# The state recurrence of a gated linear-attention branch, re-associated: factors formed for four chunks at once

## The chip, the cores and the metric

One Trainium2 chip, one of its cores. The metric is the time of one execution in microseconds of device time; the median of three runs is taken. The engines are named as the profile names them: PE is the matrix engine (PEld its weight loads), DVE the vector engine, ACT the scalar engine, POOL GpSimd, SP the queue that issues most transfers.

## The reference

A decoder layer of width 1024 over 1024 tokens. One input projection feeds three branches (a recurrence of 16 heads of 64, a causal convolution of width 31, a cross-attention into 256 tokens); each is projected, they are merged by sigmoid gates, and one output projection and a residual follow. Only the recurrence matters here:

```
def wkv7_scan(r, decay, k, v, a_vec, b_vec):
    def step(state, inp):
        r_t, w_t, k_t, v_t, a_t, b_t = inp
        sa = einsum('bhvk,bhk->bhv', state, a_t)
        state = (state * w_t[:, :, None, :] + sa[..., :, None] * b_t[:, :, None, :]
                 + v_t[..., :, None] * k_t[:, :, None, :])
        y = einsum('bhvk,bhk->bhv', state, r_t)
        return state, y
...
    wkv = wkv7_scan(rh, decay, kh, vh, -kk, kk * ah)     # then a norm per head, a bonus term, a gate
```

## The kernel before

The products of the layer ("dense" work) are 128x128 by 128x512 matmuls at line 291. Every operand is split into two parts of reduced precision, and three products of parts stand for one, so that an output tile of 128 features by 512 tokens takes 24 of them. The order in which an engine gets its instructions is chosen when the kernel is built: a scheduler starts from the order of the program and may bring ready work forward.

The recurrence is cut into units (a pair of heads j, a half e of the tokens); a unit has 8 chunks of 64 tokens. There are 16 units. Three generators work on one, each in a later period than the one ahead:

- `g_prep` (lines 454 to 549) forms decays, the scaled A and R (tile `ar`), the scaled B and K (tile `bk`) and, for each chunk, head and row, the products of `bk` with `ar` (line 541), masked by DVE at line 543 into the tile `g`. In `g` a chunk has four 64x64 blocks for each head: B with A, K with A, B with R, K with R. For even and odd chunks the halves of the 128 partitions are swapped (`own` and `oth`).
- `g_sub` (lines 552 to 613) inverts the triangular B-with-A block. The 32x32 diagonal blocks are inverted by 31 small steps on DVE (lines 575 and 578), through scratch in DRAM on both sides; two rounds of 32x32 matmuls (lines 600 and 609) make the off-diagonal block. The result T stands in `g`, in place of the block.
- `g_chain` (lines 618 to 719) walks the chunks. For four chunks at a time (q = 0, 1) it transposes `bk` (line 628, tile `tk`) and V (line 635, tile `sav`). For each chunk: line 655 multiplies the state S by A and R into a bank `ry`; line 658 adds the K-with-A block times V for each head; ACT copies this to `rhs` (661); line 669 multiplies by T; ACT copies the result beside V into `sav` (670); line 676 multiplies `tk` by `sav` for each head, and DVE makes the new state from it (679); line 683 adds the B-with-R and K-with-R blocks times `sav` for each head to `ry`, and ACT copies that to `Y` (684). The norm and the gate follow at lines 692 to 718.

A period runs a list of dense tiles (three as a rule) beside the chain of one unit, the `g_sub` of the next and the `g_prep` of the one after. `mix` (line 305) advances these generators over 60 slots, in proportion to a number of steps given for each: 12 for a dense tile (4 matmuls each), `CHN + 2 * GNW` = 30 for a chain. Accumulators are banks of PSUM: two for `d` (dense), two for `g`, two for `ry`, one for `tr`, one for `sas`.

After the last unit the attention, the convolution and the merge follow; the change does not touch them.

Of the kernel before, what the change touches and what calls it, by code (L numbers as in the profile page):

```python
# [18 lines left out]
P = 128  # L19
# [5 lines left out]
C = 64  # L25
# [4 lines left out]
CHN = 28  # L30
# [14 lines left out]
# tiles of the packed weights  # L45
# [5 lines left out]
# columns of the packed per-feature vectors  # L51
# [11 lines left out]
def hybrid_kernel(ctx: ExitStack, tc: tile.TileContext, x: bass.AP, mem: bass.AP, wt: bass.AP,  # L63
# [10 lines left out]
    def bank(tag, bufs=1):  # L74
        return ps.tile([P, HS], F32, name=tag, tag=tag, bufs=bufs)

# [35 lines left out]
    # rsqrt of (in * mul + add) on tiny tiles  # L112
# [17 lines left out]
    # weights stream through in a fixed order: load two tiles ahead, split one tile ahead  # L130
# [34 lines left out]
    # periods of the RWKV pipeline: dense tiles, and what runs beside them in which part of the period  # L165
# [17 lines left out]
    # jobs of the attention and convolution phase: a pair of GLU tiles now and then, so that the taps  # L183
    # of the convolution run beside all of it
# [47 lines left out]
    # RMSNorm of rows, transposed to [feature, token] and split  # L232
# [32 lines left out]
    # a spilled [feature, token] array, back and split  # L265
# [38 lines left out]
    # advance generators side by side; each has its number of steps and its window of the period  # L304
# [15 lines left out]
    # the first tile of products begins beside the norm of the second half of the tokens  # L320
# [7 lines left out]
    # =================== RWKV ===================  # L328
    with tc.tile_pool(name="rk", bufs=1, reuse_waits="tile") as rk:
        # Chunks of 64 tokens; chunk c keeps its own rows at partitions so = 64 * (c even) and the  # L330
        # rows of V, K, R and Y at the other half, so that two chunks fill the 128 partitions.
# [6 lines left out]
        # masks over [rows s, columns t]: strict (s < t) in the columns of A, s <= t in those of R  # L338
# [43 lines left out]
        # low-rank inputs tanh(w_lo) and a_lo: the high parts in rows 0-63, the low parts in rows 64-127  # L382
# [62 lines left out]
        # sums over the features of each head  # L445
# [8 lines left out]
        def g_prep(j, e):  # L454
# [80 lines left out]
            for par in range(2):  # L535
                for hh in range(2):
                    gp = bank("g", 2)
                    rows = slice(hh * C, (hh + 1) * C)
                    for cc in range(4):
                        c = 2 * cc + par  # L540
                        pe.matmul(gp[:, cc * P:(cc + 1) * P], lhsT=fl(bk[rows, c, :, :]), rhs=fl(ar[rows, c, :, :]),  # L541
                                  start=True, stop=True)
                    dve.tensor_tensor(out=g[:, par, hh, :, :], in0=gp.rearrange("p (c t) -> p c t", t=P),  # L543
                                      in1=cmask[par][:, None, :].broadcast_to([P, 4, P]), op=ALU.mult)
                    yield
# [6 lines left out]
        def g_sub(j, e):  # L552
            un = (2 * j + e) % 2
            g = GG[j, e]
            U = rk.tile([NG * 32, 32, 32], F32, name="U", tag="U", bufs=2)
# [28 lines left out]
            t11 = rk.tile([P, 8, 32], F32, name="t11", tag="t11")  # L584
# [33 lines left out]
        def g_chain(j, e):  # L618
# [582 lines left out]
```

## Time and profile before

| | before |
|---|---|
| median of three runs | 2046.52 us (2045.52 to 2048.74) |
| span of the profiled execution | 2042.7 us |
| PE busy | 1999.4 us, 98% of the span, 11140 matmuls |
| DVE busy | 1340.9 us, 66% |
| ACT busy | 730.0 us, 36% |
| POOL busy | 232.1 us, 11% |
| share of 16 DMA engines, main queue | 28.0% |

The span runs from the first to the last instruction of one execution that was profiled. No whole time is listed for that execution: the three timed runs are 2.8 to 6.0 us longer than its span, and that is what lies around it. A matmul's duration in the rows includes the time that it spends in the array's pipeline, so that two neighbours overlap: what one takes from the engine is read from start to start. An fp32 matmul at lines 541 to 683 appears as two instructions in the rows, a transpose or a dense product as one.

### The profile page before, as it was taken

Reading aid. Unit: us, or ns where it says so; the run is one execution under the profiler, and the core shown is the slowest. Engines: PE = TensorE matmul, PEld = TensorE weight load, DVE = VectorE, ACT = ScalarE, POOL = GpSimd, SP = SyncE. Lnnn points to the kernel's source line nnn. Section 1 sums busy time; section 2 is a strip of 40 time slices with the busy share of each in tenths; the row PEclk is TensorE's granted clock in tenths of the full one; section 3 lists DMA queues with packets and bytes.
Section 4 is the critical chain, followed back from the end, with each engine's and each line's share of the span. In section 5 each row is a group of like instructions: output and inputs, shape, how many; then the busy total and the mean of one; then the engine's idle time right before and its main releaser. Section 6 shows DMA issues by size and latency. Waiting matters only on the chain.

```text
span 2042.7 us, 29527 instructions
## 1 busy us (share of the span) xinstructions
PE 1999.4 (98%) x11140; PEld 1558.9 (76%) x11140; DVE 1340.9 (66%) x2802; ACT 730.0 (36%) x1495; POOL 232.1 (11%) x311
## 2 busy tenths in 40 slices
PE   7999999999999999999999999999999999899998
PEld 5777777777777777777777888888888777678887
DVE  6664676656667566675632798989899857654423
ACT  6324344443434434343333432332313335432221
POOL 2201201111011111111100000000000132200001
PEclk9999999999999999999999999999999999999999
DMA  4221212212121221212221432112122566795432
GB/s 141 75 79 50 63 42 59 59 50 74 28 74 43 58 65 29 78 45 65 59 63 64 155 99 62 52 52 73 62 70 75 180 212 195 227 295 176 127 133 83
DMA packets 127936, 188.59 MB, mean 92 GB/s; under 512 B 64433, under 2 KB 66609, under 8 KB 127793
## 3 DMA queue, kind: packets, MB, share of 16 engines
q1 hardware_dynamic: 122704, 178.11, 28.0%
q10 hardware_dynamic: 4768, 8.07, 1.1%
q8 instruction: 87, 1.43, 0.3%
q0 software_dynamic: 320, 0.52, 0.1%
q14 instruction: 57, 0.46, 0.1%
HBM read 139.92 MB, written 46.20 MB: 91 GB/s over the span
## 4 chain that ended last, share of the span: by engine, by line
PE 79%; DVE 9%; DMA 5%; issue 3%; ACT 2%; POOL 2%; SPq 0%; DVEq 0%; POOLq 0%; ACTq 0%
PE d L291 55%; PE d L212 4%; PE g L541 3%; PE ry L658 2%; PE sas L669 2%; DVE ac L795 2%; PE sas L676 2%; DVE wl L124 2%; DMA ost<-o_rwkv_d 1%; PE ry L683 1%; PE ry L655 1%; POOL vr L118 1%; PE g L212 1%; PE ry L212 1%; DMA wf<-in_wt_dram 1%
## 5 line engine op out<-in xcount | busy, mean ns | idle before, releaser
L291 PE MATMUL d<-hH,wh 128*128 128x512 f32 x1552 | 632.1, 407 | 5.1 <-DVE cg L882 3.6
L291 PE MATMUL d<-hH,wl 128*128 128x512 f32 x1552 | 629.8, 406 | 0.0
L291 PE MATMUL d<-hL,wh 128*128 128x512 f32 x1552 | 623.0, 401 | 0.0
L291 PEld LDWEIGHTS d<-hH,wh 128*128 128x128 f32 x1552 | 292.9, 189 | 67.0 <-DVE cg L882 4.8
L291 PEld LDWEIGHTS d<-hH,wl 128*128 128x128 f32 x1552 | 292.7, 189 | 64.6 <-issue 0.2
L291 PEld LDWEIGHTS d<-hL,wh 128*128 128x128 f32 x1552 | 293.0, 189 | 57.3
L795 DVE SCALAR_TENSOR_TENSOR ac<-up,wdw,ac 128x1024 f32<-128x1024 f32 x240 | 307.7, 1282 | 11.8 <-ACT ac L792 5.9
L123 ACT CAST wh<-wf 128x1024 fp32r<-128x1024 f32 x137 | 143.5, 1048 | 291.1 <-PE d L291 270.1
L124 DVE TENSOR_TENSOR wl<-wf,wh 128x1024 fp32r<-128x1024 f32 x137 | 170.5, 1245 | 70.1 <-ACT wh L123 70.1
L291 PE MATMUL d<-oH,wh 128*128 128x512 f32 x384 | 152.0, 396 | 9.3 <-DVE mg L1055 7.4
L679 DVE SCALAR_TENSOR_TENSOR s<-sas,pc,sp 64x64 f32<-64x64 f32 x240 | 67.9, 283 | 130.2 <-PE sas L676 125.9
L291 PE MATMUL d<-oL,wh 128*128 128x512 f32 x384 | 151.1, 393 | 0.0
L291 PE MATMUL d<-oH,wl 128*128 128x512 f32 x384 | 150.8, 393 | 0.0
L575 DVE TENSOR_TENSOR tm<-W,U 128x60 f32<-128x60 f32 (+24 forms) x496 | 112.0, 226 | 21.8 <-POOL W L568 5.5
L578 DVE TENSOR_TENSOR W<-W,tm 128x60 f32<-128x60 f32 (+24 forms) x496 | 106.0, 214 | 13.1 <-POOL W L568 0.6
L543 DVE TENSOR_TENSOR g<-g,cmask 128x512 f32<-128x512 f32 x64 | 44.2, 691 | 99.6 <-PE g L541 99.0
L291 PEld LDWEIGHTS d<-oH,wh 128*128 128x128 f32 x384 | 72.4, 189 | 28.4 <-DVE mg L1055 6.3
L291 PEld LDWEIGHTS d<-oH,wl 128*128 128x128 f32 x384 | 72.5, 189 | 15.9
L291 PEld LDWEIGHTS d<-oL,wh 128*128 128x128 f32 x384 | 72.5, 189 | 15.4
L541 PE MATMUL g<-ar,bk 64*128 64x128 f32 x512 | 77.6, 291 | 1.5 <-POOL bk L525 1.5
L670 ACT COPY sav<-sas 64x128 f32<-64x128 f32 x128 | 33.4, 261 | 124.3 <-PE sas L669 123.8
L684 ACT COPY Y<-ry 64x128 f32<-64x128 f32 x128 | 33.1, 259 | 123.8 <-PE ry L683 121.4
(271 smaller groups left out, 2737.2 us busy)
## 6 DMA issues: line engine op xcount, KB each, us to landing
wf<-in_wt_dram SPq DMA_DIRECT2D x137, 512.0 KB
g_d<-gt SPq DMA_DIRECT2D x48, 256.0 KB
U<-ud SPq DMA_DIRECT2D x64, 128.0 KB
nxt<-in_x_dram SPq DMA_DIRECT2D x8, 512.0 KB
o_rwkv_d<-o SPq DMA_DIRECT2D x16, 256.0 KB
cv_d<-ac SPq DMA_DIRECT2D x8, 512.0 KB
o_mem_d<-om SPq DMA_DIRECT2D x16, 256.0 KB
xs<-cv_d SPq DMA_DIRECT2D x8, 512.0 KB
```

The costliest lines, as they stand in the source:

```text
L123: act.copy(hi, src)
L124: (eng or dve).tensor_tensor(out=lo, in0=src, in1=hi.bitcast(F32), op=ALU.subtract)
L212: pe.matmul(po, lhsT=l, rhs=r, start=(i == 0), stop=(i == n - 1))
L291: pe.matmul(po, lhsT=l[:, ks_], rhs=r[:, k, sl], start=(n == 0), stop=(n == 3 * KT - 1))
L541: pe.matmul(gp[:, cc * P:(cc + 1) * P], lhsT=fl(bk[rows, c, :, :]), rhs=fl(ar[rows, c, :, :]), start=True, stop=True)
L543: dve.tensor_tensor(out=g[:, par, hh, :, :], in0=gp.rearrange("p (c t) -> p c t", t=P), in1=cmask[par][:, None, :].broadcast_to([P, 4, P]) ...
L575: dve.tensor_tensor(out=tv, in0=W[:, 0:m, i:i + 1].broadcast_to([NG * 32, m, n]), in1=U[:, i:i + 1, i + 1:32].broadcast_to([NG * 32, m, n] ...
L578: dve.tensor_tensor(out=wv_, in0=wv_, in1=tv, op=ALU.add)
L658: pe.matmul(ry[own, vsl], lhsT=gc[oth, hh, own], rhs=sav[oth, cc, vsl], start=False, stop=(hh == 1))
L669: pe.matmul(sa[own, vsl], lhsT=gc[own, hh, own], rhs=rhs[own, vsl], start=True, stop=True)
L679: dve.scalar_tensor_tensor(out=S1[vsl, vsl], in0=sn[vsl, 0:C], scalar=pc[vsl, c:c + 1], in1=sp[vsl, vsl], op0=ALU.mult, op1=ALU.add)
L795: dve.scalar_tensor_tensor(out=ac, in0=up[:, tap:tap + S], scalar=wdw[:, tap * 8 + j:tap * 8 + j + 1], in1=ac, op0=ALU.mult, op1=ALU.add)
```

## The change

- `g_sub` no longer writes the inverse into `g`. The inverted diagonal blocks are loaded into a tile `wb`, and their transposes by DVE (four of 32x256, before two) go into a new tile `TT`, which holds T transposed; the two rounds of 32x32 matmuls make its off-diagonal block and now alternate between the two partition halves. `U` has one buffer, before two.
- A new generator `g_pre` does, for four chunks, the two transposes as before, then T'B (into `tk`, in place of B), K-with-A times V (into `Y`), and T'(B-with-R) (into `g`, in place of the block): 24 matmuls of 64x64x64, whose order alternates between partition halves and between two banks. ACT copies the results out.
- A chunk's step is `ry` = S times A and R (128x128x128, four chunks share a bank); DVE adds the K-with-A term from `Y` and writes the sum beside V into `sav`; `sn` = `tk` times `sav` (128x128x128, of which the two diagonal 64x64 blocks are used); DVE makes the new state as before. The copies to `rhs` and of `sa` and the matmuls with T are gone from it.
- After four chunks the output is formed together: 8 matmuls of 128x64x64 into a bank `tr`, one copy by ACT into `Y`, two additions of the R rows of `ry` by DVE, and the statistics.
- `g_pre` of the second four chunks runs in the first three steps of the first four. `CHN` is 23, before 28.
- In `g_prep` the matmuls of the two heads alternate (rows 0 to 63, rows 64 to 127), into two banks, and both masks follow; before, one head's products and its mask came ahead of the other's.

The diff without edits of comments, cut to its core:

```diff
-CHN = 28
+CHN = 23
...
+        TT = rk.tile([P, 8, C], F32, name="TT")
+        for r in (0, C):
+            dve.memset(TT[r:r + 32, :, 32:C], 0.0)
...
             for par in range(2):
+                gps = [bank("g", 2) for _ in range(2)]
+                for cc in range(4):
+                    c = 2 * cc + par
+                    for hh in range(2):
+                        rows = slice(hh * C, (hh + 1) * C)
+                        pe.matmul(gps[hh][:, cc * P:(cc + 1) * P], lhsT=fl(bk[rows, c, :, :]),
+                                  rhs=fl(ar[rows, c, :, :]), start=True, stop=True)
...
-            U = rk.tile([NG * 32, 32, 32], F32, name="U", tag="U", bufs=2)
+            U = rk.tile([NG * 32, 32, 32], F32, name="U", tag="U", bufs=1)
...
+                    nc.sync.dma_start(out=wb[rows], in_=wd[un][b, par::2].rearrange("i s t -> s i t"))
+            for par in range(2):
+                for b in range(2):
+                    rows = slice(so(par) + b * 32, so(par) + (b + 1) * 32)
+                    dve.transpose(out=TT[rows, :, b * 32:(b + 1) * 32], in_=wb[rows])
...
+            for i in range(8):
+                for par in range(2):
+                    r0 = so(par)
+                    r1 = r0 + 32
+                    pe.matmul(zp[r1:r1 + 32, i * 32:(i + 1) * 32], lhsT=g[r0:r1, par, i // 4, i % 4, r1:r1 + 32],
+                              rhs=TT[r0:r1, i, 0:32], start=True, stop=True)
...
+        def g_pre(j, e, q, g, bk, v, Y):
...
+            zv = vtp[:, 2 * P:4 * P]
+            u1 = bank("g", 2)
+            uv = u1.rearrange("p (k c h t) -> p k c h t", k=2, c=2, h=2)
+            for n in range(4):
+                cc2, hh = n // 2, n % 2
+                vsl = slice(hh * C, (hh + 1) * C)
+                for par in range(2):
+                    own = slice(so(par), so(par) + C)
+                    oth = slice(ko(par), ko(par) + C)
+                    cc = cc2 * 2 + par
+                    gc = g[:, par, hh, q * 2 + cc2]
+                    pe.matmul(uv[own, 0, cc2, hh, :], lhsT=TT[own, hh * 4 + q * 2 + cc2, :], rhs=tk[own, cc, vsl],
+                              start=True, stop=True)
+                    pe.matmul(zv[own, n * C:(n + 1) * C], lhsT=gc[oth, own], rhs=sav[oth, cc, vsl],
+                              start=True, stop=True)
+            for n in range(4):
...
+                    pe.matmul(uv[own, 1, cc2, hh, :], lhsT=TT[own, hh * 4 + q * 2 + cc2, :],
+                              rhs=g[own, par, hh, q * 2 + cc2, oth], start=True, stop=True)
+            act.copy(fl(Y[:, q * 2:q * 2 + 2, :]), zv)
+            for par in range(2):
+                own = slice(so(par), so(par) + C)
+                oth = slice(ko(par), ko(par) + C)
+                act.copy(tk[own, par::2, :], uv[own, 0].rearrange("p c h t -> p c (h t)"))
+                act.copy(g[own, par, :, q * 2:q * 2 + 2, oth], uv[own, 1].rearrange("p c h t -> p h c t"))
...
+                    pe.matmul(ry[:, cs], lhsT=fl(ar[:, c, :, :]), rhs=S0, start=True, stop=True)
+                    dve.tensor_tensor(out=sav[own, cc, :], in0=ry[own, cs], in1=Y[own, c // 2, :], op=ALU.add)
...
-                    sa = bank("sas")
-                    for hh in range(2):
-                        vsl = slice(hh * C, (hh + 1) * C)
-                        pe.matmul(sa[own, vsl], lhsT=gc[own, hh, own], rhs=rhs[own, vsl], start=True, stop=True)
-                    act.copy(sav[own, cc, :], sa[own, 0:P])
-                    yield
...
                         sn = bank("sas")
+                        pe.matmul(sn[:, 0:P], lhsT=tk[:, cc, :], rhs=sav[:, cc, :], start=True, stop=True)
...
+                yp = bank("tr")
+                for n in range(4):
+                    cc2, hh = n // 2, n % 2
+                    for par in range(2):
+                        oth = slice(ko(par), ko(par) + C)
+                        pe.matmul(yp[oth, n * C:(n + 1) * C], lhsT=g[:, par, hh, q * 2 + cc2, oth],
+                                  rhs=sav[:, cc2 * 2 + par, hh * C:(hh + 1) * C], start=True, stop=True)
+                act.copy(fl(Y[:, q * 2:q * 2 + 2, :]), yp[:, 0:2 * P])
```

## Rows read from the trace of the kernel before

**Rows 1.** The page, its part on the chain of work that ended last: shares of the span by engine.

```profile
PE 79%; DVE 9%; DMA 5%; issue 3%; ACT 2%; POOL 2%; SPq 0%; DVEq 0%; POOLq 0%; ACTq 0%
```

**Rows 2.** Busy time by stretch: the recurrence from its first chain to its last, and a stretch of the attention and convolution. Columns: stretch in us, its length, then busy us and instructions of PE, PEld, DVE, ACT and POOL, the granted TensorE clock as a share of 2.4 GHz, the DMA share and GB/s.

```profile
130.00:1130.00 1000.00, 994.48 (x6466) 731.81 (x6467) 606.30 (x1875) 391.92 (x951) 127.84 (x188) 0.99 0.20 57
...
1200.00:1600.00 400.00, 399.92 (x1882) 334.52 (x1881) 358.92 (x372) 115.93 (x216) 18.72 (x13) 1.00 0.20 65
```

**Rows 3.** Waits from 130 to 1130 us, PE's list and the first of DVE's: who waited for whom, us in total, times, longest.

```profile
PE tr L713 <- DVE Y L708: 4.5, 7, 1.6
...
DVE s L679 <- PE sas L676: 125.9, 92, 7.3
```

**Rows 4.** The line that clears the state for a new pair of heads: durations, then first and last start of its 7 later uses (from the second pair of heads to the eighth). Six pairs of units lie between.

```profile
L622 DVEq EVENT_SEMAPHORE  x7: 21/21/21, 239.1 to 983.8; - x7
```

**Rows 5.** PE's timeline over one chunk's step, from one use of line 655 to the next: start in us, length of the group, what ran, count. The lines left out are dense matmuls, one to a line. In all 18 matmuls of 512 columns lie between the two uses of line 655 (lines 450 and 451, and 4, 8 and 4 of line 291).

```profile
408.94 0.38 PE L655 MATMUL ry<-s,ar 128*128 128x128 f32 x2
409.26 0.44 PE L658 MATMUL ry<-sav,g 64*64 64x64 f32 x4
409.63 0.50 PE L450 MATMUL g<-hsh,bones 128*128 128x512 f32 x1
409.96 0.39 PE L451 MATMUL g<-hsl,bones 128*128 128x512 f32 x1
...
410.89 0.40 PE L291 MATMUL d<-hH,wl 128*128 128x512 f32 x1
411.22 0.44 PE L669 MATMUL sas<-rhs,g 64*64 64x64 f32 x4
411.59 0.50 PE L291 MATMUL d<-hH,wh 128*128 128x512 f32 x1
411.93 0.39 PE L291 MATMUL d<-hL,wh 128*128 128x512 f32 x1
...
413.64 0.34 PE L676 MATMUL sas<-sav,tk 128*64 128x64 f32 x4
413.80 0.40 PE L683 MATMUL ry<-sav,g 128*64 128x64 f32 x4
414.13 0.50 PE L291 MATMUL d<-hH,wl 128*128 128x512 f32 x1
...
415.18 0.38 PE L655 MATMUL ry<-s,ar 128*128 128x128 f32 x2
```

**Rows 6.** The same view a little earlier: four full-array fp32 transposes of 128 columns between dense matmuls.

```profile
406.09 0.39 PE L291 MATMUL d<-hH,wl 128*128 128x512 f32 x1
406.32 0.60 PE L628 MATMUL tr<-ident,bk 128*128 128x128 f32 x4
406.68 0.48 PE L291 MATMUL d<-hH,wh 128*128 128x512 f32 x1
406.99 0.40 PE L291 MATMUL d<-hL,wh 128*128 128x512 f32 x1
```

**Rows 7.** The same view in a later unit: a group of 32x32 matmuls, and the products of one head between dense matmuls.

```profile
553.54 0.69 PE L600 MATMUL tr<-t,g 32*32 32x32 f32 x16
554.16 0.93 PE L541 MATMUL g<-ar,bk 64*128 64x128 f32 x6
...
564.29 0.40 PE L291 MATMUL d<-hL,wh 128*128 128x512 f32 x1
564.61 1.16 PE L541 MATMUL g<-ar,bk 64*128 64x128 f32 x8
565.70 0.50 PE L291 MATMUL d<-hH,wl 128*128 128x512 f32 x1
566.03 0.39 PE L291 MATMUL d<-hH,wh 128*128 128x512 f32 x1
```

**Rows 8.** Groups of instructions by line over one pair of units (239 to 363.2 us, DVE) and, last, over the first 1000 us (ACT): count, busy us, mean ns of one, idle time before them and what ended it.

```profile
L679 DVE SCALAR_TENSOR_TENSOR s<-sas,pc,sp 64x64 f32<-64x64 f32 x30 | 8.5, 283 | 11.3 <-PE sas L676 10.9
L124 DVE TENSOR_TENSOR wl<-wf,wh 128x1024 fp32r<-128x1024 f32 x6 | 7.3, 1218 | 0.3 <-ACT wh L123 0.3
L543 DVE TENSOR_TENSOR g<-g,cmask 128x512 f32<-128x512 f32 x8 | 5.5, 691 | 12.7 <-PE g L541 12.6
...
L591 DVE STREAM_TRANSPOSE t<-g 32x256 f32<-32x256 f32 x4 | 1.7, 433 | 0.8 <-DMA g<-wd 0.7
...
L644 ACT COPY sav<-tr 64x256 f32<-64x256 f32 x56 | 20.6, 367 | 8.3 <-PE tr L635 7.6
```

**Rows 9.** The same pair of units by stretch (columns as in rows 2): the six of twelve equal stretches in which DVE is busiest, and the pair as a whole.

```profile
249.30:259.70 10.40, 10.27 (x98) 7.50 (x99) 7.94 (x16) 3.42 (x7) 4.21 (x3) 1.00 0.13 31
...
270.00:280.30 10.30, 10.30 (x60) 7.57 (x59) 8.80 (x30) 4.49 (x10) 0.00 (x0) 1.00 0.15 52
280.30:290.70 10.40, 10.40 (x63) 7.61 (x62) 9.55 (x35) 6.27 (x14) 1.54 (x3) 1.00 0.00 1
...
332.00:342.30 10.30, 10.30 (x63) 7.56 (x60) 8.32 (x30) 4.77 (x11) 1.59 (x2) 1.00 0.12 40
342.30:352.70 10.40, 10.40 (x62) 7.71 (x61) 8.11 (x34) 3.57 (x10) 1.90 (x2) 1.00 0.26 78
352.70:363.00 10.30, 10.30 (x70) 7.77 (x69) 7.82 (x32) 3.42 (x9) 0.00 (x0) 1.00 0.29 83
...
239.00:363.00 124.00, 123.50 (x819) 90.77 (x819) 81.19 (x252) 50.13 (x122) 17.74 (x26) 1.00 0.20 55
```

More of the change, by code (lines that the diff above doesn't have):

```diff
@@ L535, in g_prep @@
             for par in range(2):
-                for hh in range(2):
[L537 to L543, printed above, removed]
+                gps = [bank("g", 2) for _ in range(2)]
[5 more added lines that the diff above has]
+                                  rhs=fl(ar[rows, c, :, :]), start=True, stop=True)
+                for hh in range(2):
+                    dve.tensor_tensor(out=g[:, par, hh, :, :], in0=gps[hh].rearrange("p (c t) -> p c t", t=P),
                                       in1=cmask[par][:, None, :].broadcast_to([P, 4, P]), op=ALU.mult)
@@ L603, in g_sub @@
+            for par in range(2):
+                r1 = so(par) + 32
+                act.copy(fl(zt[r1:r1 + 32]), zp[r1:r1 + 32, 0:256])
             yield
             zp2 = bank("tr")
[L605 to L612 removed]
+            for i in range(8):
+                for par in range(2):
+                    r1 = so(par) + 32
+                    pe.matmul(zp2[r1:r1 + 32, i * 32:(i + 1) * 32], lhsT=wb[r1:r1 + 32, i, :],
+                              rhs=zt[r1:r1 + 32, i, :], start=True, stop=True)
@@ L674, in g_chain @@
                         for hh in range(2):
                             vsl = slice(hh * C, (hh + 1) * C)
-                            pe.matmul(sn[vsl, 0:C], lhsT=tk[:, cc, vsl], rhs=sav[:, cc, vsl], start=True, stop=True)
-                        for hh in range(2):
-                            vsl = slice(hh * C, (hh + 1) * C)
-                            dve.scalar_tensor_tensor(out=S1[vsl, vsl], in0=sn[vsl, 0:C], scalar=pc[vsl, c:c + 1],
+                            dve.scalar_tensor_tensor(out=S1[vsl, vsl], in0=sn[vsl, vsl], scalar=pc[vsl, c:c + 1],
@@ L680, in g_chain @@
                                                      in1=sp[vsl, vsl], op0=ALU.mult, op1=ALU.add)
-                    for hh in range(2):
-                        vsl = slice(hh * C, (hh + 1) * C)
-                        pe.matmul(ry[oth, vsl], lhsT=gc[:, hh, oth], rhs=sav[:, cc, vsl], start=False, stop=(hh == 1))
-                    act.copy(Y[oth, c // 2, :], ry[oth, 0:P])
-                    if par:
-                        for hh in range(2):
-                            vsl = slice(hh * C, (hh + 1) * C)
-                            dve.bn_stats(out=st[:, c // 2, hh, :], in_=Y[:, c // 2, vsl])
@@ L689, in g_chain @@
-                    state[0] = 1 - state[0]
-                    yield
+                        state[0] = 1 - state[0]
+                    if q == 0 and cc < 3:
+                        got = next(pre[1])
+                    yield
+                yp = bank("tr")
+                for n in range(4):
+                    cc2, hh = n // 2, n % 2
+                    for par in range(2):
+                        oth = slice(ko(par), ko(par) + C)
+                        pe.matmul(yp[oth, n * C:(n + 1) * C], lhsT=g[:, par, hh, q * 2 + cc2, oth],
+                                  rhs=sav[:, cc2 * 2 + par, hh * C:(hh + 1) * C], start=True, stop=True)
@@ new lines, in g_chain @@
+                act.copy(fl(Y[:, q * 2:q * 2 + 2, :]), yp[:, 0:2 * P])
+                yield
+                ryv = ry.rearrange("p (c t) -> p c t", t=P)
+                for par in range(2):
+                    oth = slice(ko(par), ko(par) + C)
+                    dve.tensor_tensor(out=Y[oth, q * 2:q * 2 + 2, :], in0=Y[oth, q * 2:q * 2 + 2, :],
+                                      in1=ryv[oth, par::2, :], op=ALU.add)
+                for c2 in range(q * 2, q * 2 + 2):
+                    for hh in range(2):
+                        dve.bn_stats(out=st[:, c2, hh, :], in_=Y[:, c2, hh * C:(hh + 1) * C])
```

82 lines of the change are left out of this document (34 added, 48 removed).

## The prediction

> **What bounds the kernel now.** I read the chain of waits first: 79% of it is PE's own work [rows 1]. Then the busy time by stretch: from 130 to 1130 us, where the recurrence runs, PE is busy 994 of 1000 us, DVE 606 and ACT 392 [rows 2]. The waits agree: PE's own list there is led by 4.5 us, while DVE waits 125.9 us for the state product of PE alone [rows 3]. So in this stage every microsecond that PE is spared shortens the time, until DVE, which has 39% to spare, becomes the bound. The later stage runs the same work as before and I count it at nothing. From 239.1 to 983.8 us there are six pairs of units [rows 4]: 124.1 us a pair, 62.05 us a unit, 16 units in all.
>
> **The price of a step on PE.** PE's timeline from start to start shows it. A dense matmul takes 0.2325 us (409.96 to 410.89, four of them) [rows 5]. One chunk's step runs from 408.94 to 415.18, 6.24 us, with 18 dense matmuls (4.19 us) in it; the step itself takes **2.05 us** [rows 5]. Where does that go? The four small instructions of line 669 stand between dense starts at 410.89 and 411.93: 1.04 us, less two dense ones 0.575 us. Groups of 16 instructions of 32 columns start 0.62 us apart [rows 7], so a small instruction costs little; line 683's four take 0.33 us with the way out [rows 5]. I read some 0.058 us for an instruction of 64 columns in one place of the array, 0.23 us for four, and the other **0.34 us** as the price of leaving the full array and coming back. A step pays it three times. Full-array fp32 instructions don't pay it: four of 128 columns stand between dense starts at 406.09 and 406.99, 0.90 us less two dense ones, 0.435 us, **0.11 us each** [rows 6].
>
> **The change, part by part (PE, a unit).**
>
> The step. It becomes two full-array fp32 matmuls of two instructions: 4 x 0.11 = 0.44 us against 2.05. Eight steps: -12.9 us.
>
> `g_pre`. For each four chunks 24 matmuls of 64x64, 48 instructions, and one way out and back (0.34). What one instruction costs where the place in the array alternates is shown by line 676 alone: its two heads write different column halves, and its four instructions take 0.16 us to the start of line 683, whose four, all in one column half, take 0.33 [rows 5]. So two places work side by side. Bounds: 0.058 each (2.8 us) if nothing overlaps, a quarter of that (0.7 us) if all four 64x64 places do. I take half, 1.4, since line 676 shows two. Twice (1.4 + 0.34): +3.5 us (2.1 to 6.2). The transposes in it are those of before.
>
> The output for four chunks: 16 instructions with alternating column halves, as line 676: 0.46 + 0.34, twice: +1.6 us (2.5 without overlap).
>
> Products in `g_prep`. One head's eight instructions stand between 564.29 and 566.03: 1.74 us, less two dense ones 1.275 [rows 7], of which eight at 0.112 are 0.90 and 0.38 the way out and back. Four such groups become two of sixteen: 0.77 us less in any case, 2.55 if the row halves work side by side. No row shows row halves together; I take the middle, -1.7 us.
>
> The off-diagonal block. Four groups of 16 now follow two sets of transposes; if pairs stay together, two ways out and back go (0.68), and overlap could halve the 64 instructions of 0.032 (from 0.69 us for 16 with a tail) for another 1.0 [rows 7]. From 0 to -1.7; I take -1.2.
>
> Sum on PE: -12.9 + 3.5 + 1.6 - 1.7 - 1.2 = **-10.7 us a unit**, bounds -5.0 and -13.4; 16 units: -171 us (-80 to -215).
>
> **What DVE takes back.** DVE gets eight additions of 64x128 from PSUM. The nearest rows are 64 columns at 283 ns and 512 at 691 [rows 8], so some 0.34 us: 2.7. Four additions of 256 columns at 0.46: 1.8. Two more transposes at 0.433: 0.9. In all 5.4 us more on 40.6 (81.2 a pair [rows 9]): 46.0 us a unit, against 51.35 for PE. On the mean DVE fits; in places it doesn't, and the step now hands work to DVE twice, so PE can't run far ahead of it. I take the twelve stretches of the pair. PE's share shrinks to 51.35/62.05 = 0.828, 8.5 us a stretch; DVE's grows by 0.9. In the six rows shown DVE then wants 8.8, 9.7, 10.45, 9.2, 9.0 and 8.7 [rows 9], beyond PE by 4.6 us together; the others are below PE's or at it. Seven full pairs: +32 us. From 0, if the scheduler moves DVE's work apart, to more in a rival below.
>
> **What else moves.** ACT loses 24 copies of a step and gets 12 larger ones (five in a row at 0.367 [rows 8] behind `g_pre`); it stays under half busy. The first `sn` waits for those copies: at most 5 x 0.367 = 1.8 us a unit, at best nothing, since a head sum, the first `ry` and a slot's dense work stand between. I take 0.5: +8 us. Bank `tr` is used nine times a unit, before seven, and held longer by `g_pre`; PE's only listed wait for it was 4.5 us in the whole stage [rows 3], and I put what is new in those 0 to 1.8 us. SP has as many transfers as before, and nothing is moved past it: `wb` is loaded where `g` was. The single buffer of `U` makes its load wait for the last step of the inverse of the unit ahead, which is done before the period ends; if it were not, the weight loads queued behind it on SP would wait too.
>
> -171 + 32 + 8 = -131 us. On the span: 2042.7 - 131 = 1911.7; the median of the runs lies 3.8 us above it: **1916 us**.
>
> **A rule against the overlap.** The Trainium skill, TensorEngine Tiling (Array Packing), section "Restrictions and Gotchas", says that different row tiles can't access the same PSUM bank at the same time. In `g_pre` the even and odd chunks of one product use different row halves and write one bank, and so do the two halves of the 32x32 rounds. No row of this trace has such a pair; line 676's pair shares its rows. By that rule the sum would be that of the second rival.
>
> **The rivals.**
>
> 1. DVE becomes the bound of the whole unit. In the attention stage it reaches 90% beside a full PE (359 of 400 us) [rows 2], but there with independent work; here it is at 61% now. At 80%, between them, 46.0 us of work takes 57.5: 4.55 us a unit less than now, -73 us, **1974 us**. For it: DVE is already at 9.55 of 10.4 us in one stretch [rows 9]. Against it: its largest wait is for a product of PE that now comes sooner [rows 3].
>
> 2. Row halves that write one bank go one after another. `g_pre` costs 6.2, the rounds gain only the 0.68, the products (two banks) gain 2.55: -12.9 + 6.2 + 1.6 - 2.55 - 0.68 = -8.3 us a unit, -133; DVE then takes back 2.5 a pair, +18, and the copies +8: -107, **1940 us**.
>
> 3. DVE answers the steps late. The addition into `sav` and the state's update stand in DVE's queue among instructions of up to 1.2 us (line 124 [rows 8]), and PE waits in order. Between two hand-overs lie some 1.3 us of dense work (144 dense matmuls over 25 slots), which covers one such instruction. The gain is gone at 163/128 = 1.3 us of uncovered wait a step; two uncovered instructions a step (2.4 us x 128 = 307) would give **2191 us**. Against it: the update at line 679 already stands there and PE's list has no wait for it [rows 3].
>
> 4. The change does not do what it says: PE pays a way out and back for each full fp32 matmul too (0.34 x 2 x 128 = 87 us). Rows 6 speak against it, though for transposes only. With the rest as forecast, -44 us, **2003 us**.
>
> **How the numbers follow.** The forecast's case (1870 to 1935) 0.44, rival 1 (1950 to 1990) 0.24, rival 2 0.18, rival 3 0.05, rival 4 0.04, no change 0.02, and 0.03 for a gain near PE's own bound with nothing taken back (below 1870). The range reaches to rival 1's time and, below, to PE's -171 with nothing taken back: 1870 to 1985. A measurement of this kernel can tell about 0.2% from no change; faster by more 0.93, within 0.02, slower 0.05.
>
> **What would show it.** Right: a unit of 53 to 54 us; a step as two groups of two instructions without a gap around them; line 676's successor at 0.22 us; `g_pre` at some 1.7 us for 48 instructions; DVE at 85% in the stage. Wrong: PE with waits for DVE's addition or the state's update (rivals 1 and 3); instructions of `g_pre` 0.058 us apart (rival 2); dense starts 0.3 us after `ry` (rival 4). A granted clock that falls more often than now (0.99 in the stage [rows 2]) would raise every term.

## The result, and the profile after

The changed kernel takes **1961.2 us** (median of 4 runs, 1959.39 to 1961.86) against 2047.63 us of the kernel before beside it (2045.52 to 2053.81). The ratio is 0.9574, with a 95% interval of 0.9558 to 0.9589: 86 us faster. The forecast was 1916, its range 1870 to 1985. So direction and range held, and 45 us of the 131 did not come: the time lies in the band of rival 1 (1950 to 1990), not in that of the forecast's case (1870 to 1935).

The page of the changed kernel: the busy time, and two groups of the new step (busy us, mean ns of one, idle time ahead and what ended most of it). Its chain of work that ended last is followed only part of the way and adds up to 40% of the span, so I don't read it against [rows 1].

```profile
PE 1848.2 (94%) x11412; PEld 1472.8 (75%) x11412; DVE 1411.1 (72%) x3028; ACT 693.2 (35%) x1303; POOL 226.5 (12%) x311
...
L710 PE MATMUL sas<-sav,tk 128*128 128x128 f32 x240 | 54.1, 307 | 34.1 <-DVE sav L703 32.4
...
L703 DVE TENSOR_TENSOR sav<-ry,Y 64x128 f32<-64x128 f32 x128 | 36.8, 288 | 43.4 <-ACT Y L668 26.5
```

PE falls from 98% of the span to 94%, and a new idle time of 34.1 us stands ahead of the state's product (line 710; `sn` in the code, tile `sas` in the rows), nearly all of it until DVE's addition of line 703 is done. The same stretch as in [rows 2], from the first chain to the last:

```profile
130.00:1043.00 913.00, 845.32 (x6714) 646.20 (x6713) 678.93 (x2122) 354.63 (x757) 123.41 (x188) 0.99 0.22 63
```

PE is idle for 913.0 - 845.3 = 67.7 us of the stage, before for 5.5 us. DVE is busy for 74% of it, not for the 85% that I expected to see. PE's list of waits there, against the single entry of 4.5 us in [rows 3]:

```profile
PE sas L710 <- DVE sav L703: 32.4, 43, 1.8
PE tr L759 <- DVE Y L754: 19.1, 6, 3.3
PE tr L759 <- DVE W L583: 6.2, 6, 1.0
PE ry L702 <- DVE s L713: 5.8, 13, 0.9
```

**The step as it was meant to be** (PE's timeline; start, length, what ran; compare [rows 5]):

```profile
458.47 0.39 PE L291 MATMUL d<-hH,wl 128*128 128x512 f32 x1
458.70 0.38 PE L710 MATMUL sas<-sav,tk 128*128 128x128 f32 x2
458.84 0.48 PE L291 MATMUL d<-hH,wh 128*128 128x512 f32 x1
459.16 0.40 PE L291 MATMUL d<-hL,wh 128*128 128x512 f32 x1
...
459.62 0.40 PE L291 MATMUL d<-hH,wh 128*128 128x512 f32 x1
459.86 0.46 PE L702 MATMUL ry<-s,ar 128*128 128x128 f32 x2
460.07 0.48 PE L291 MATMUL d<-hL,wh 128*128 128x512 f32 x1
```

From 458.47 to 459.16 there are 0.69 us, less two dense matmuls at 0.2325: 0.225 us for the product, 0.11 an instruction, and no way out of the array; `ry` takes 460.07 - 459.62 - 0.2325 = 0.22. A step with nothing late costs 0.45 us where it cost 2.05.

**The step as it is in many places** (the same view of PE, then DVE's timeline over the same time):

```profile
429.00 0.38 PE L702 MATMUL ry<-s,ar 128*128 128x128 f32 x2
429.14 0.48 PE L291 MATMUL d<-hH,wl 128*128 128x512 f32 x1
429.45 0.39 PE L291 MATMUL d<-hH,wh 128*128 128x512 f32 x1
429.68 0.40 PE L291 MATMUL d<-hL,wh 128*128 128x512 f32 x1
429.92 0.39 PE L291 MATMUL d<-hH,wl 128*128 128x512 f32 x1
430.63 0.49 PE L710 MATMUL sas<-sav,tk 128*128 128x128 f32 x2 [0.33 <-DVE sav L703]
```

```profile
429.08 1.22 DVE L486 TENSOR_TENSOR_SCAN lw<-rmask,lw 128x512 f32<-128x512 f32 x1
...
430.30 0.28 DVE L703 TENSOR_TENSOR sav<-ry,Y 64x128 f32<-64x128 f32 x1
```

`ry` has long been there, but the addition comes behind a scan of 1.22 us in DVE's queue. PE has four dense matmuls to put in between, 0.93 us; they run out, and the product starts late, with all dense work queued behind it in order.

**The norm's tail** (PE, then DVE, then POOL):

```profile
418.98 0.63 PE L759 MATMUL tr<-ident,Y 128*128 128x128 f32 x4 [3.17 <-DVE Y L754]
```

```profile
416.01 2.82 DVE L754 TENSOR_TENSOR Y<-Y,vr 128x512 f32<-128x512 f32 x1 [1.10 <-POOL vr L118]
```

```profile
415.94 2.34 POOL L574 TENSOR_TENSOR U<-U,rb 128x1024 f32<-128x1024 f32 x1
```

The norm's product on DVE takes 2.82 us in place of 0.69 whenever POOL's product of `U` (line 574) runs beside it; it ends 0.55 us after POOL's does (418.83, 418.28). That is so in 6 of 16 units, and PE waits up to 3.3 us there, 19.1 us in all; in most of the others it waits some 1.0 us at the same place. In all units together that is 27.1 us. The kernel before has such products too (7 of 16, up to 2.87), but PE has dense work left behind each of the seven and does not idle there: the 4.5 us of [rows 3] stand in the units in which the product takes 0.69. Now PE's transposes are called for sooner.

Behind the stall the granted clock falls to half (columns as in [rows 2]; the last value but two is the clock's share of 2.4 GHz):

```profile
415.70:419.20 3.50, 0.33 (x3) 0.25 (x3) 2.82 (x1) 0.00 (x0) 2.58 (x2) 1.00 0.00 0
419.20:422.60 3.40, 3.40 (x16) 2.80 (x15) 1.50 (x2) 0.87 (x2) 0.00 (x0) 0.59 0.16 61
```

PE, idle for 3.2 of the 3.5 us ahead, runs the next 3.4 us at 0.59 on the mean, so for most of them at the lower of its two levels, 1.2 GHz. Such a stretch follows five of the six stalls of 3.2 us.

**The ledger.** Summed over PE's instructions from start to start, from the first state product to the end of the last chunk's matmuls (before) or to the last state product (after):

```
                          before  137.0 to 1116.7   after  137.3 to 1024.6
total                     979.7 us                  887.3 us
times PE leaves the full array   441                   134
late starts ahead of sn, ry and
  the two sets of transposes      11                    85
lost to half clock                 7                     8.5
the rest: PE's own work          961.7                 793.8
```

A late start is what a product's distance from the instruction ahead of it exceeds the shortest such distance in the trace. Time at half clock, 13.7 us before and 17.1 after, counts by half. PE's own work fell by 168 us in these two stretches. They do not hold the same work: 2328 matmuls of line 291 before and 2301 after, and to the first matmul of line 212, where the next stage begins, it is 29.7 us more before and 34.7 after. So 5 of the 168 us are work that was only moved behind the stretch; like for like PE's own work fell by some **163 us**, and the forecast's sum was 171. Of the 85 us, 38 stand between a dense matmul and `sn`, some 28 ahead of the norm's transposes, 10.6 ahead of `ry`, and 8 between a transpose of `bk` and `sn`. A further 4 us of the span are lost outside the stage, nearly all of them behind it.

### The profile page after: what moved, and what is told of

It reads as the page before. It is cut to its first block, busy times and chain, and to the rows that moved or that the text cites. A ratio compares the mean times of both kernels' runs of the same rounds, so it can differ in the third digit from the quotient of the medians.

```text
span 1959.0 us, 30018 instructions
## 1 busy us (share of the span) xinstructions
PE 1848.2 (94%) x11412; PEld 1472.8 (75%) x11412; DVE 1411.1 (72%) x3028; ACT 693.2 (35%) x1303; POOL 226.5 (12%) x311
## 5 line engine op out<-in xcount | busy, mean ns | idle before, releaser
L291 PE MATMUL d<-hH,wl 128*128 128x512 f32 x1552 | 621.8, 401 | 0.0
L124 DVE TENSOR_TENSOR wl<-wf,wh 128x1024 fp32r<-128x1024 f32 x137 | 176.8, 1291 | 95.7 <-ACT wh L123 95.4
L583 DVE TENSOR_TENSOR W<-W,tm 128x60 f32<-128x60 f32 (+24 forms) x496 | 112.4, 227 | 10.0
L580 DVE TENSOR_TENSOR tm<-W,U 128x60 f32<-128x60 f32 (+24 forms) x496 | 107.7, 217 | 11.1
L706 ACT ACTIVATE sp<-s,pc 128x128 f32<-128x128 f32 x120 | 48.3, 402 | 174.8 <-DVE s L713 137.6
L710 PEld LDWEIGHTS sas<-sav,tk 128*128 128x128 f32 x240 | 38.4, 188 | 67.5 <-DVE sav L703 49.2
L710 PE MATMUL sas<-sav,tk 128*128 128x128 f32 x240 | 54.1, 307 | 34.1 <-DVE sav L703 32.4
L703 DVE TENSOR_TENSOR sav<-ry,Y 64x128 f32<-64x128 f32 x128 | 36.8, 288 | 43.4 <-ACT Y L668 26.5
```

What stands on the lines that cost most here:

```text
L124: (eng or dve).tensor_tensor(out=lo, in0=src, in1=hi.bitcast(F32), op=ALU.subtract)
L291: pe.matmul(po, lhsT=l[:, ks_], rhs=r[:, k, sl], start=(n == 0), stop=(n == 3 * KT - 1))
L580: dve.tensor_tensor(out=tv, in0=W[:, 0:m, i:i + 1].broadcast_to([NG * 32, m, n]), in1=U[:, i:i + 1, i + 1:32].broadcast_to([NG * 32, m, n] ...
L583: dve.tensor_tensor(out=wv_, in0=wv_, in1=tv, op=ALU.add)
L703: dve.tensor_tensor(out=sav[own, cc, :], in0=ry[own, cs], in1=Y[own, c // 2, :], op=ALU.add)
L706: act.activation(sp, S0, AF.Copy, scale=pc[:, c:c + 1])
```

## The experiments

The theories. The letters changed their sense from one set of runs to the next, so each expectation is to be read by its own words. **A**: the hand-over to PE waits in DVE's queue behind other work (e1, e2), or DVE has too much to do whatever lies between (e4, e6, e7; rival 1 in the form of the forecast's twelve stretches). **B**: the bare turn-around PE, DVE, PE, DVE is too long even with a free DVE (in e5: no change). **C**: a question of distance, more dense work ahead of the product that waits covers it (e4, e6, e7); in e10 and e12 C says that the order in DVE's queue makes no difference. **D**: DVE's part of the step put ahead of its other work shortens the wait. All kernels are the changed one with the edit shown, unless the text says otherwise.

**e1: half of the inverse's steps left out.**

```diff
-            for i in range(31):
+            for i in range(0, 31, 2):
...
-                if i % 2:
-                    yield
+                yield
```

> The changed kernel with every second of the 31 steps of the inverse of a 32x32 block left out (lines 580 and 583), so that the inverse is incomplete: 30 small DVE instructions of some 0.22 us less in a unit, 6.6 us, none of them in the step from chunk to chunk. Theory A, the step waits in DVE's queue behind other work (from the end of the state product on PE to the start of DVE's addition 1.50 us pass on the mean, 1.27 of them with DVE at other instructions): PE's idle time in the stage, 67.7 us after against 5.5 before, mostly goes, 1890 to 1915 us. Theory B, PE waits for the bare turn-around of a step (PE, DVE, PE, DVE), which is as long with a free DVE: 1946 us or more.

Measured: 1938.63 us (1935.79 to 1941.29), ratio 0.9467 (0.9448 to 0.9487): 23 us faster than the change. The stage, with DVE busy for 615 us in place of 679, and PE's waits:

```profile
130.00:1020.00 890.00, 830.24 (x6749) 647.81 (x6748) 615.16 (x1647) 358.17 (x759) 130.74 (x188) 0.98 0.23 64
```

```profile
PE sas L709 <- DVE sav L702: 26.3, 38, 2.4
PE tr L758 <- DVE Y L753: 20.5, 7, 3.0
PE ry L701 <- DVE s L712: 10.8, 15, 1.8
```

It fell between the two expectations. The waits of PE hardly shrink (59.8 us idle), though DVE is idle for 275 of 890 us. I read it so that other work moves up and stands ahead of the additions in place of the inverse; no run shows that by itself. Load counts for something; it is not what sets the waits.

**e2: the addition on PE and ACT.** K V is copied into `sav` and added by a product with the identity, and ACT copies the sum; DVE has nothing to do between `ry` and `sn`. The lines left out make the identity's tile `idp`, copy the K-with-A term into `sav`, and put `zt` into the buffer of `W`.

```diff
...
+                    pe.matmul(ry[:, cs], lhsT=idp[:, par, :], rhs=sav[:, cc, :], start=True, stop=False)
-                    pe.matmul(ry[:, cs], lhsT=fl(ar[:, c, :, :]), rhs=S0, start=True, stop=True)
-                    dve.tensor_tensor(out=sav[own, cc, :], in0=ry[own, cs], in1=Y[own, c // 2, :], op=ALU.add)
+                    pe.matmul(ry[:, cs], lhsT=fl(ar[:, c, :, :]), rhs=S0, start=False, stop=True)
+                    act.copy(sav[own, cc, :], ry[own, cs])
```

> The changed kernel with the sum of a step moved from DVE: the K-with-A term is put into sav, PE adds it into the bank of the state product with one more full-array fp32 matmul (by an identity, two instructions), and ACT copies the sum to sav. PE gets 0.22 us a step more, 28 us in all, DVE 0.29 us less, ACT 0.26 us more. Theory A: the step leaves DVE's queue once, PE's 34 us of idle time ahead of the second product go, and with them what its successors lose; 1925 to 1955 us. Theory B: a turn-around over ACT is as long, so that only the 28 us of PE work show; 1975 to 1990 us.

Measured: 1980.0 us (1978.79 to 1981.01), ratio 0.9671 (0.965 to 0.9692), slower than the change by 19, within the range of B. PE's waits:

```profile
PE tr L767 <- DVE Y L762: 26.3, 7, 3.8
PE ry L710 <- DVE s L721: 24.3, 35, 1.4
PE sas L718 <- ACT sav L711: 20.8, 28, 1.3
```

The wait ahead of `sn` is shared with ACT's own queue, and the state's update by DVE, whose wait was 5.8 us, now costs 24.3. The hand-over was taken from DVE and the time was not; 128 more products on PE (some 0.22 us each by the step's rows) come on top.

**e3: the kernel before, with the two heads' products alternating alone.**

```diff
+                gps = [bank("g", 2) for _ in range(2)]
+                for cc in range(4):
+                    c = 2 * cc + par
+                    for hh in range(2):
+                        rows = slice(hh * C, (hh + 1) * C)
+                        pe.matmul(gps[hh][:, cc * P:(cc + 1) * P], lhsT=fl(bk[rows, c, :, :]),
+                                  rhs=fl(ar[rows, c, :, :]), start=True, stop=True)
...
```

> The kernel before with one part of the change alone: the matmuls of the two heads in the preparation alternate between rows 0 to 63 and rows 64 to 127 and write two banks. PE is the bound there, so what PE saves shows in full. If row halves work side by side, 2.55 us a unit, 41 us in all: 2006 us. If they don't, two ways out of the full array and back a unit, 0.77 us, 12 us in all: 2034 us.

Measured: 2037.86 us (2035.01 to 2039.04), ratio 0.995 (0.9931 to 0.9969): 11 us faster than before, 0.5%. By the time alone the row halves would not work side by side (2034); the trace says otherwise. By the ledger the products fell from 63.9 to 33.4 us, so PE was spared 30 us, the bound of full overlap; 20 went back at one place:

```profile
PE tr L714 <- DVE Y L709: 25.1, 16, 3.2
```

The norm's tail, 4.5 us in [rows 3], costs 25.1 here, with the recurrence as it was. PE got to the transposes earlier, and DVE did not. The wait comes in every unit: 10.9 us in the seven whose product takes 2.8 us beside POOL's, 14.2 us in the nine whose product takes 0.69.

**e4: more steps around the norm.** `GNW`, the number of steps given up on either side of the norm's two DVE instructions, from 1 to 4. The chain's number of steps rises with it, from 25 to 31.

```diff
-GNW = 1
+GNW = 4
```

> The changed kernel with four slots instead of one ahead of each half of the norm's tail (GNW 4), so that the transposes of the normalised output come later in PE's order. PE idles 26 us ahead of them in the changed kernel (3.2 us at 415.8 us, while DVE's last product of the norm takes 2.82 us in place of 0.69 beside a POOL product), and a granted clock of one half follows for 3.4 us. Theory C (distance): that idle time goes, 1930 to 1945 us. Theory A: DVE is late for whatever comes next, and the idle time moves to the next step, 1955 us or more.

Measured: 1939.22 us (1937.72 to 1940.34), ratio 0.9455 (0.9435 to 0.9476), 22 us faster than the change, as C expected. The wait ahead of the norm's transposes is gone from PE's list, and part of it came back elsewhere, as A expected: 22.0 us ahead of `sn` (32.4) and 21.9 ahead of `ry` (5.8) lead the list now. The edit did two things at once, for the norm's product no longer meets POOL's (its uses in e4; minimum, median and maximum in ns, first and last start):

```profile
L754 DVE TENSOR_TENSOR Y<-Y,vr x16: 691/692/694, 176.5 to 1010.6; 128x512 f32<-128x512 f32 x16
```

POOL's product now runs beside DVE's work for the preparation: at 416.8 us line 480 takes 2.44 us in place of 0.43, and PE then idles 0.82 us ahead of `sn` and 2.09 ahead of `ry`. Which of the two took the wait away, e9 tells.

**e9: POOL's product of U on DVE**, 1.22 us there in place of 2.38 on POOL.

```diff
-            pool.tensor_tensor(out=U, in0=U, in1=rb[:, None, :].broadcast_to([NG * 32, 32, 32]), op=ALU.mult)
+            dve.tensor_tensor(out=U, in0=U, in1=rb[:, None, :].broadcast_to([NG * 32, 32, 32]), op=ALU.mult)
```

> The changed kernel with the product of U and the row scales (2.34 us on POOL, one a unit) on DVE instead (some 1.2 us). If DVE stands still while POOL runs that product (2.82 us in place of 0.69 for the norm's last product in six of sixteen units), DVE loses less than it gets, PE's wait ahead of the output's transposes shrinks from 26 us to some 12, and the time is 1945 to 1958 us. If DVE's load is what counts, 19 us of work more show: 1965 to 1980 us.

Measured: 1952.3 us (1951.73 to 1955.09), ratio 0.9524 (0.9506 to 0.9543): 9 us faster, within the expected time. The norm's product takes 0.69 us in all units, against up to 2.82 in the changed kernel (the line's uses in e9, then two of PE's waits):

```profile
L754 DVE TENSOR_TENSOR Y<-Y,vr x16: 691/692/694, 182.6 to 1026.9; 128x512 f32<-128x512 f32 x16
```

```profile
PE sas L710 <- DVE sav L703: 23.6, 45, 1.2
PE tr L759 <- DVE Y L754: 14.4, 8, 1.8
```

The expected reason failed: PE's waits ahead of the norm's transposes add up to 24.3 us (27.1 in the changed kernel), not to 12. They are shorter and come in more units, at most 1.8 us (3.3). So the collision alone is not what makes PE wait there; what took the wait away in e4 is the slots. The gain stands elsewhere: PE idles 61 us in all (68), and no part of the stage runs at half clock (17.1 us in the changed kernel, 8.5 us lost). DVE got 16 x 1.22 us of work more, and the kernel became faster. That speaks against DVE's load as the limit more plainly than e1.

**e5: the other way, more work on POOL.** In the stage the low parts of the weights are formed on POOL.

```diff
+    stream.eng = pool
...
+    stream.eng = dve
```

> The changed kernel with the subtraction that makes the low part of a weight tile moved from DVE to POOL in the recurrence's stage (three of 1.24 us a unit, 3.7 us of DVE's time, none in the step). Theory A: DVE's queue is shorter and the step waits less, 1925 to 1945 us; less of a gain, or none, if DVE stands still while POOL runs (DVE instructions of 0.2 us lasted 0.6 to 0.7 beside a POOL product in the kernel before). Theory B: no change, 1955 to 1965 us.

Measured: 2092.64 us (2089.29 to 2097.75), ratio 1.0222 (1.0198 to 1.0246): slower than the kernel before, which no expectation had. The stage:

```profile
130.00:1178.00 1048.00, 896.11 (x6721) 683.49 (x6721) 706.27 (x2073) 356.45 (x757) 245.59 (x238) 0.93 0.20 55
```

With 49 instructions fewer DVE is busy for longer (706 against 679 us): what is left runs slower beside POOL; the norm's product takes 2.8 us in 13 of 16 units (6). PE is idle for 152 us of the stage, and the mean clock falls to 0.93.

**e6 and e7: a second slot between `ry` and `sn`** (C), alone and with `GNW` 4; the chain's number of steps is raised for it.

```diff
-CHN = 23
+CHN = 31
...
                         act.activation(sp, S0, AF.Copy, scale=pc[:, c:c + 1])
+                    yield
                     yield
```

> The changed kernel with one more slot of the interleaving between the state product and the second product of each step (one more yield, CHN 31), nothing else. Theory C: the loss is a question of distance: where four dense matmuls (0.93 us) lie between the two products PE idles 0.4 us on the mean, where eight lie, 0.01; so 34 us of idle time ahead of the second product fall below 10, and the time to 1925 to 1945 us. Theory A (DVE's queue is too long whatever lies between): idle time stays, within 8 us of 1961. It would be slower if the steps, now closer to the end of the unit, run into the next one.

> The two edits of distance together (one more slot in the step, CHN 31, and GNW 4). Theory C: both idle times go, 60 us of 66, 1890 to 1915 us, and DVE is busy over 85% of the stage. Theory A: no better than the better of the two.

Measured: e6 2007.93 us (2005.6 to 2009.28), ratio 0.9792 (0.9773 to 0.981), slower than the change by 47; e7 1968.1 us (1959.55 to 1971.84), ratio 0.9593 (0.9564 to 0.9622), 29 us slower than e4. PE's waits of e6, and its norm's product:

```profile
PE tr L760 <- DVE Y L755: 53.6, 15, 3.9
PE ry L702 <- DVE s L714: 27.3, 36, 1.6
PE sas L711 <- DVE sav L703: 16.3, 28, 0.9
...
L755 DVE TENSOR_TENSOR Y<-Y,vr x16: 691/2818/2826, 184.2 to 1082.5; 128x512 f32<-128x512 f32 x16
```

The wait ahead of `sn` was halved, from 32.4 to 16.3; C had said below 10. `ry` and the norm lost more than that. The step's slots were taken from the other hand-overs, as I read it; but in e6 the norm's product also meets POOL's in 13 of 16 units (6), so e6 alone doesn't tell the two apart. e7 does: there no unit's norm meets POOL's product and the norm's wait is gone, PE waits 28.5 us ahead of `ry` and 21.1 ahead of `sn`, and the second slot still costs 29 us against e4. As a way to a faster kernel C fell for the step.

**e10: DVE's part of the step first** (D). The scheduler is told to prefer the addition and the two state updates.

```diff
+                    with tc.high_priority(offset=400):
+                        dve.tensor_tensor(out=sav[own, cc, :], in0=ry[own, cs], in1=Y[own, c // 2, :], op=ALU.add)
-                    dve.tensor_tensor(out=sav[own, cc, :], in0=ry[own, cs], in1=Y[own, c // 2, :], op=ALU.add)
...
```

> The changed kernel with DVE's three instructions of a step (the addition into sav, the two of the state) put ahead of other ready work when the order of the engines is fixed, nothing else. Theory D, the order in DVE's queue: in the 74 steps in which PE was late for the second product, DVE began the addition 2.34 us after the state product's end and spent 1.95 us of that on other instructions; with the step ahead of them the idle time at the step (40 us) at least halves, 1930 to 1945 us. Theory C, the bare turn-around is longer than four dense matmuls: the idle time stays, 1955 us or more.

Measured: 1970.64 us (1969.17 to 1973.25), ratio 0.9617 (0.9601 to 0.9633), 9 us slower than the change. The wait ahead of `sn` is still 30.6 us (32.4). The edit hardly moved the additions: the median from the end of `ry` to the addition's start is 0.84 us (0.90). So this run doesn't test D's mechanism; it shows that the edit alone doesn't bring it about.

**e11: e4 and e9 together, and e12: e11 with e10's edit.**

> The changed kernel with four slots ahead of each half of the norm's tail and the product of U on DVE (the two edits that gained, 22 us and 9 us). If they take away different waits, 1928 to 1935 us; if the second worked only by the norm's product that the first has already covered, 1937 to 1945 us.

> The same with DVE's instructions of a step ahead of other ready work. Theory D: the idle time that is left ahead of the second product and of the state product (some 45 us with the norm covered) at least halves, 1900 to 1915 us. Theory C: no better than without, 1928 us or more.

Measured: e11 **1907.99 us** (1907.68 to 1910.23), ratio 0.9316 (0.9302 to 0.933). It is below both expected ranges. It beats both kernels, the changed one by 53 us, and it comes out where the forecast had put the change. The stage and PE's waits of e11, then those of e12:

```profile
130.00:990.00 860.00, 824.01 (x6698) 636.53 (x6697) 668.19 (x2136) 351.18 (x754) 98.90 (x174) 1.00 0.24 66
```

```profile
PE sas L710 <- DVE sav L703: 19.5, 30, 1.1
PE ry L702 <- DVE s L713: 12.3, 22, 0.8
```

```profile
PE sas L711 <- DVE sav L704: 9.5, 18, 1.1
PE ry L702 <- DVE s L715: 7.8, 18, 0.8
```

In e11 PE is idle for 36 us of the stage (67.7), late starts take 49.6 us (85), and no time is left at half clock (17.1 us). So the ledger shows 35.4 + 8.5 = 44 of the 53 us. The two edits had given 22 and 9 alone, and I had expected no more than their sum. Each alone left what the other takes away: e9 the norm's wait, e4 the collisions, now with other DVE work. From e4 to e11, 31 us apart, late starts fall from some 64 us to 49.6 and the time at half clock from 23.9 us to nothing, 12 us; how much of that is POOL's product is not shown.

e12 takes 1928.26 us (1926.95 to 1934.4), ratio 0.9419 (0.9401 to 0.9436). The wait ahead of `sn` halved, the additions start 0.44 us after `ry` in the median (0.69), and late starts fell from 49.6 to 39.8 us, as D says; and yet it is 20 us slower than e11, where C had put it: the scheduler placed the rest differently too, and PE leaves the full array 163 times, in e11 126. At 0.34 us each that is 13 us.

## Why the prediction was right, and where it was short

**The range: held by luck.** Its upper part was drawn for rival 1, and the time fell into that rival's band. The rival's mechanism did not come: it had DVE busy for 80% as the bound of the unit, while DVE is busy for 74% of the stage and the kernel gets faster with more work on it (e9).

**What PE is spared: right.** Some -163 against -171 us. Its terms, by groups between dense matmuls on PE's timeline of the changed kernel:

```profile
456.24 0.40 PE L291 MATMUL d<-hL,wh 128*128 128x512 f32 x1
456.57 1.16 PE L545 MATMUL g<-ar,bk 64*128 64x128 f32 x16
457.66 0.51 PE L291 MATMUL d<-hH,wl 128*128 128x512 f32 x1
458.01 0.40 PE L291 MATMUL d<-hH,wh 128*128 128x512 f32 x1
...
470.13 0.69 PE L618 MATMUL tr<-zt,wb 32*32 32x32 f32 x32
471.55 0.40 PE L291 MATMUL d<-hH,wh 128*128 128x512 f32 x1
471.88 0.69 PE L724 MATMUL tr<-sav,g 128*64 128x64 f32 x16
472.49 0.50 PE L291 MATMUL d<-hL,wh 128*128 128x512 f32 x1
472.83 0.40 PE L291 MATMUL d<-hH,wl 128*128 128x512 f32 x1
...
490.31 0.64 PE L666 MATMUL g<-g,TT 64*64 64x64 f32 x16
```

- The step: 0.45 us, forecast 0.44. Rival 4 (a way out for each full fp32 matmul) is refuted by the rows of the step above.
- The products: sixteen instructions in 1.77 - 0.465 = 1.305 us; before eight took 1.275. That is the bound of 2.55 us a unit, where I took the middle, 1.7.
- The output: 1.28 - 0.465 = 0.815 us against 0.80.
- `g_pre`: 16 instructions in 0.64 us. A single one of 64 columns takes some 0.22 in the pipeline, so they start (0.64 - 0.22) / 15 = 0.028 us apart, half of 0.058, as I took it. Its 48 instructions take 1.58 us with the way back to come, against 1.74 in all.
- The rounds: 32 instructions in the 0.69 us that 16 took [rows 7].

So **rival 2 is refuted**: in `g_pre` and in the rounds both row halves write one bank, each its own partitions, and they run side by side: in line 666's group the two of a pair start 0.013 us apart, and the next pair 0.058 us after the first. The Trainium skill's sentence on row tiles and PSUM banks (TensorEngine Tiling (Array Packing), "Restrictions and Gotchas") doesn't hold for these products; the measurement decides.

**What DVE takes back: the step that failed.** I put 32 us there from twelve stretches of DVE's busy time, and 8 for the hand-over of copies. The ledger has 74 more of late starts (85 less 11) and 1.5 of half clock in the stage, and 4 are lost outside of it. With the 8 us that PE's sum missed, the difference to the forecast is 35.5 + 4 + 8 = 47.5; by the spans it is 1959.0 - 1911.7 = 47.3. The term that was mis-sized is this one: 74 us of late starts where 40 stood.

It was mis-sized because it asked the wrong thing. DVE's own cost was below what I counted: 0.288 us for the addition (0.34), and some 73 us more in the stage (678.9 against 606.3 [rows 2]) where I had 5.4 x 16 = 86. At 74% it is not the bound (rival 1), and e9 gave it work and won time. What counts is when a hand-over comes, at two places:

1. *The step's cover.* I wrote that 1.3 us of dense work lie between two hand-overs; that is a mean. By the four commonest counts of dense matmuls between `ry` and `sn`:

```
dense matmuls between   steps   mean idle ahead of sn, us
4 (0.93 us)              39      0.40
5 (1.16 us)               8      1.25
6 (1.40 us)              26      0.19
8 (1.86 us)              19      0.01
```

The eight steps with five are the longest waits, so the count alone doesn't set them; in e6, 39 steps with eight dense matmuls and nothing else between still idle for 0.34 us on the mean. DVE starts the addition 1.50 us after `ry` on the mean (0.90 in the median), and is at other work for 1.13 of these; the 1.27 in e1's expectation counts overlapping instructions twice. What stands ahead of the addition counts too: in one of the eight, ahead of the `sn` at 440.98 us, the addition comes behind DVE instructions of 1.22 and 0.69 us (lines 124 and 527). This is rival 3's mechanism, the answer late behind instructions of up to 1.2 us. I gave it 0.05 at a price of 2.4 us a step; it holds in part, at 0.38 us over the 120 second products (46 us). It should have been a term of the sum. I took the absence of a wait for line 679 in [rows 3] as evidence against it; as I read it now, PE, with 2.05 us of its own work in each step, had hidden it then.

2. *The norm's tail.* It isn't in the forecast at all: I read "4.5 us" in [rows 3] as the size of that wait, and it was the size of what PE's slowness left visible. e3 shows it with the recurrence unchanged (25.1). What makes PE wait there is that its transposes are called for too soon: with more slots the wait is gone (e4), without the collision it stays (e9). What the collision with POOL's product adds is single stalls of 3.2 us and the half clock behind them. The Trainium skill, SBUF — State Buffer, section "Who interferes with whom", says that a VectorE instruction with two SBUF inputs contends with a GpSimd instruction that reads SBUF, and that the ports that they share are "an exclusive lock". The trace agrees: the norm's product starts 0.07 us after POOL's, takes 2.82 us in place of 0.69, and ends 0.55 us after it. The kernel before had the same rows, and I didn't read them.

Shown by runs: that the norm's wait was hidden by PE's own work before (e3) and is a matter of slots (e4, e9), that waits move to the next hand-over when one is covered or taken from DVE (e2, e4, e6, e7), and that DVE's volume isn't the limit (e1, e9). Only in part shown: that the wait ahead of `sn` comes from what stands ahead of the addition in DVE's queue; e12 halves it by order, e10's edit did not change the order enough to tell. Open: how much of the 49.6 us of late starts still in e11 can be ordered away. e12 cut 10 of them and lost more elsewhere.

## What to carry to other kernels

Price small matmuls by how often PE leaves the full array, not by their columns: 0.34 us each time here, and 441 times became 134. When PE is spared work in a program of fixed queues, go through every product that waits for another engine and compare the cover at each place, not the mean, with the longest instruction that can stand ahead of the answer; a small wait in the trace of before may be one that PE's own work still hides. Then look at what the answering engine shares a stretch with: moving one POOL product and giving the norm more slots gave back 53 us here, more than the forecast was short by.

## What was not expected of the hardware

- A DVE product of 128x512 in SBUF takes 0.69 us alone and 2.82 beside a POOL product of 128x1024; giving POOL more (e5) made the kernel slower by 131 us.
- Matmuls in different row halves that write different partitions of one bank run side by side: 0.028 us apart on the mean, against 0.058.
- A stall of 3.2 us costs PE more than itself in five of six cases: at the one shown the granted clock is 0.59 on the mean over the next 3.4 us.
